# One accumulator per MLP tile, no weight remainders or norm squares on GpSimd, and another cost model for the order of the instructions

## The chip, the cores and the metric

The kernel runs on one core of one Trainium2 chip. The metric is the device time of one execution in microseconds (us), the median of several runs. A core has a matmul engine (TensorE, PE in the profile; its weight loads are shown apart as PEld), three engines for elementwise work (VectorE = DVE, ScalarE = ACT, GpSimd = POOL) and SyncE (SP), which here issues DMAs.

## The reference

The reference is a decoder trunk of two layers on 256 tokens of width 1024, in fp32:

```python
for layer in range(2):
    h = rms_norm(x, mix_norm[layer])
    if layer == 0:   # gated DeltaNet (8 heads x 64) beside a short gated convolution (512 channels)
        x = x + gdn_shortconv_mixer(h, w_in, qkv_conv, a_log, dt_bias, o_norm, sc_conv, w_out)
    else:            # native sparse attention, 16 heads, 4 key groups, three gated branches
        x = x + nsa_mixer(h, w_in, cmp_pos, k_w1, k_w2, v_w1, v_w2, w_out)
    h = rms_norm(x, mlp_norm[layer])
    x = x + square(relu(h @ w_up[layer])) @ w_down[layer]     # 1024 -> 4096 -> 1024
return rms_norm(x, final_norm)
```

The DeltaNet mixer projects, convolves q, k and v over time (width 4), applies SiLU, normalises q and k per head, inverts a triangular matrix per chunk and scans over chunks. The attention mixer projects, rotates a quarter of each head, compresses blocks of keys and values by a small MLP, and runs softmax over compressed, selected and window keys.

## The kernel before

**Weights and products.** All weights come as one stream of 108 MB or so, mostly in transfers of 1 MB, issued by SP into four slots called `st` (line 407). Each unit of a transfer (128 x 1024, in layer 0 also 512 and 528, for values 560) is split in two: ScalarE copies its high part `uh` (in the fp32r format that PE takes), and VectorE or GpSimd subtracts to get the exact remainder `ul` (`splits`, lines 443 to 451). Four buffers hold split units. X, the normalised input `x` and the MLP's hidden `U` are held as such pairs too. A product is then hi·xh + hi·xl + lo·xh. There are two forms of it. `mm256` issues three matmuls of 256 columns into one accumulator. `mm512` issues one matmul of 512 columns (xh and xl side by side) that fills both halves of a bank, and one of 256 columns for lo·xh; the two halves are added when the tile is evacuated (`addab`, line 623: ScalarE copies one half to `tb`, VectorE adds).

**Stages.** In the trace the layer-0 mixer takes 0 to 210 us, its MLP 210 to 381, the layer-1 mixer 381 to 553, its MLP 553 to 726, and the final norm and the store the rest. An MLP computes 32 up tiles (the first four contraction outermost in `proj_ko`, 28 one after the other in `proj_m`), then 8 down tiles of 32 products each. Its norm's factor is applied at the end: the square of it, `r2`, multiplies the down tiles.

**Norms.** When a tile of X is done, `Norm.ready` makes the pair `x`, squares the tile (`sq`, by ScalarE or GpSimd) and adds it to `nacc` (VectorE or GpSimd); `Norm.finish` sums over partitions by matmuls with `ones` and gets 1/rms.

**What sets the order.** Every engine runs its instructions in program order, and that order is made when the kernel is built. The work is written as generators (streams); the class `Order` always lets the stream go on that could start first by its clock. The clock goes by costs from `Timed.cost` (PE) and `Timed.other` (others), by a delay after each engine (`LAG`), and by a rule that doubles PE's cost after a stretch with few matmul columns (`TICK`, `BUSY`). Where a stream may choose an engine, the estimated end decides, with a bias in ns: `GB1` (first 16 units) and `GBIAS` favour GpSimd for remainders, `QBIAS` for squares. The costs are estimates for the order alone. All instructions but the DMAs issued at line 407 carry the line of the helper that records them, 279 before and 294 after.

## Time and profile before

| | |
|---|---|
| median of 3 runs | 741.78 us (738.81 to 750.28) |
| the profiled execution: span on the chip | 737.2 us |
| its own time | not recorded apart from the three runs; the median lies 4.6 us above its span |
| PE busy | 684.5 us in 5613 matmuls |
| DVE / ACT / POOL busy | 555.7 / 352.3 / 216.0 us |
| DMA | 108.94 MB, mean 148 GB/s |

The span is divided by engine and by stage in the rows below. Busy times add up over an engine's instructions; idle time on PE is what the stages differ in. The granted clock (PEclk) is given as a share of full speed, 1.00 for 2.4 GHz and 0.50 for 1.2 GHz.

### The profile page before, as it was taken

What the parts mean: (1) busy time and instruction counts of PE and PEld (TensorE: products, weight loads), DVE (VectorE), ACT (ScalarE), POOL (GpSimd) and SP (SyncE); (2) the same over time, 40 slices, a digit from 0 to 9 for tenths busy, and PEclk for the clock granted to TensorE, in tenths of its full rate; (3) what the DMA queues carried; (4) which work ended last, traced back from release to release, by engine and by line L of the source; (5) the groups of instructions that cost most, each with busy time, mean ns of one, the idle gap of its engine ahead of it and who ended that gap; (6) DMA issues with size and microseconds to landing.
All of it is one profiled execution on the core that took longest, in us unless ns stands there. A gap on an engine that the chain in (4) does not pass through costs nothing.

```text
span 737.2 us, 13951 instructions
## 1 busy us (share of the span) xinstructions
PE 684.5 (93%) x5613; PEld 602.5 (82%) x5613; DVE 555.7 (75%) x1007; ACT 352.3 (48%) x681; POOL 216.0 (29%) x229
## 2 busy tenths in 40 slices
PE   8878979999999999999999799888989999999994
PEld 6877878898888888888898677876778888888884
DVE  6999976676898887666679987798598888754552
ACT  6353423242656565444446647445655656544430
POOL 3536786512520000012143455342361000011211
PEclk9999999999999999999999989999999999999998
DMA  8552323113545554554552347412134555555401
GB/s 281 209 179 108 130 68 110 60 59 115 172 160 187 203 193 172 186 208 178 175 174 89 106 156 239 162 58 62 60 128 153 179 209 183 176 191 204 173 0 58
DMA packets 17633, 108.94 MB, mean 148 GB/s; under 512 B 2080, under 2 KB 2336, under 8 KB 5536
## 3 DMA queue, kind: packets, MB, share of 16 engines
q1 hardware_dynamic: 17280, 107.52, 41.8%
q8 instruction: 44, 0.72, 0.4%
q10 hardware_dynamic: 288, 0.52, 0.2%
q14 instruction: 21, 0.17, 0.1%
HBM read 106.99 MB, written 1.05 MB: 147 GB/s over the span
## 4 chain that ended last, share of the span: by engine, by line
PE 72%; DVE 22%; issue 3%; ACT 2%; DMA 1%; SPq 0%; POOL 0%; DVEq 0%; ACTq 0%
PE b L279 72%; DVE ul L279 4%; DVE cvconv L279 2%; DVE cm L279 1%; DVE rqt L279 1%; DVE x L279 1%; ACT uh L279 1%; DVE tt L279 1%; DVE qr L279 1%; DVE swq L279 1%; DMA X<-xt 1%; DVE nacc L279 1%; DVE X L279 1%; DVE ncol L279 1%; DVE qrot L279 1%
## 5 line engine op out<-in xcount | busy, mean ns | idle before, releaser
L279 ACT ACTIVATE uh<-st 128x1024 fp32r<-128x1024 f32 (+3 forms) x204 | 205.4, 1011 | 235.2 <-PE b L279 214.6
L279 PE MATMUL b<-x,uh 128*128 128x256 f32 (+1 forms) x1120 | 304.4, 348 | 1.7 <-DVE x L279 1.4
L279 DVE TENSOR_TENSOR ul<-st,uh 128x1024 fp32r<-128x1024 f32 (+3 forms) x166 | 205.3, 1238 | 102.5 <-ACT uh L279 101.5
L279 PE MATMUL b<-x,ul 128*128 128x256 f32 x832 | 227.1, 285 | 2.5 <-DVE ul L279 2.5
L279 PEld LDWEIGHTS b<-x,uh 128*128 128x128 f32 x1120 | 193.1, 195 | 24.3 <-DVE x L279 2.2
L279 PE MATMUL b<-U,uh 128*128 128x512 f32 (+1 forms) x576 | 179.8, 371 | 0.0
L279 PEld LDWEIGHTS b<-x,ul 128*128 128x128 f32 x832 | 160.9, 193 | 8.9 <-DVE ul L279 3.3
L279 PE MATMUL b<-U,ul 128*128 128x256 f32 x512 | 141.5, 281 | 0.0
L279 PEld LDWEIGHTS b<-U,uh 128*128 128x128 f32 x576 | 103.1, 188 | 19.5
L279 POOL TENSOR_TENSOR ul<-st,uh 128x1024 fp32r<-128x1024 f32 (+3 forms) x38 | 77.6, 2045 | 71.9 <-ACT uh L279 69.8
L279 PEld LDWEIGHTS b<-U,ul 128*128 128x128 f32 x512 | 96.1, 188 | 1.3
L279 POOL TENSOR_TENSOR nacc<-nacc,sq 128x256 f32<-128x256 f32 x24 | 28.8, 1200 | 70.3 <-ACT sq L279 69.3
L279 DVE TENSOR_TENSOR t<-b,tb 128x256 f32<-128x256 f32 x82 | 34.3, 418 | 0.1
L279 POOL TENSOR_TENSOR X<-X,par 128x256 f32<-128x256 f32 x8 | 5.6, 703 | 97.7 <-ACT nacc L279 90.5
L279 ACT ACTIVATE tb<-b 128x256 f32<-128x256 f32 x82 | 30.0, 369 | 7.6 <-PE b L279 6.5
L279 POOL TENSOR_TENSOR nacc<-X 128x256 f32<-128x256 f32 x2 | 1.2, 614 | 101.3 <-DVE X L279 101.3
L279 DVE SCALAR_TENSOR_TENSOR u<-t 128x256 f32<-128x256 f32 x64 | 29.2, 456 | 2.2
L279 ACT ACTIVATE px<-b,nm 128x128 f32<-128x128 f32 (+1 forms) x64 | 26.1, 429 | 8.9 <-DVE nm L279 8.8
L279 DVE TENSOR_TENSOR U<-u,U 128x256 fp32r<-128x256 f32 x64 | 28.2, 446 | 1.1 <-ACT U L279 1.1
L279 ACT ACTIVATE U<-u 128x256 fp32r<-128x256 f32 x64 | 25.7, 404 | 6.3 <-DVE u L279 6.2
L279 POOL TENSOR_TENSOR sq<-X 128x256 f32<-128x256 f32 x13 | 9.9, 765 | 64.0 <-DVE X L279 57.4
L279 DVE SCALAR_TENSOR_TENSOR x<-X,par,x 128x256 fp32r<-128x256 f32 x32 | 25.7, 831 | 3.6 <-ACT x L279 3.5
(277 smaller groups left out, 920.5 us busy)
## 6 DMA issues: line engine op xcount, KB each, us to landing
st<-wts SPq DMA_DIRECT2D x94, 1024.0 KB, 4.8
st<-wts SPq DMA_DIRECT2D x4, 560.0 KB, 3.7
st<-wts SPq DMA_DIRECT2D x4, 528.0 KB, 4.4
st<-wts SPq DMA_DIRECT2D x8, 256.0 KB, 5.8
X<-xt SPq DMA_DIRECT2D x3, 256.0 KB, 5.9
par<-par SPq DMA_DIRECT2D x1, 525.0 KB, 6.1
out_dram<-X SPq DMA_DIRECT2D x2, 256.0 KB, 2.5
out_dram<-X ACTq DMA_DIRECT2D x2, 256.0 KB, 3.1
```

The costliest lines, as they stand in the source:

```text
L279: r = f(*a, **k)
```

## The change

**MLP tiles.** Up and down tiles use `mm256` (three matmuls of 256 columns, one accumulator) throughout. An up tile was evacuated by a copy on ScalarE, an add and a relu-square on VectorE, the high part on ScalarE and the remainder on VectorE; now ScalarE does relu, square and high part, and VectorE the remainder alone. A down tile loses its copy and its add.

**GpSimd.** The choice of engine goes: remainders `ul` are always VectorE's, high parts and squares always ScalarE's. Thirty-eight remainders move from GpSimd to VectorE, thirteen squares and two first sums from GpSimd to ScalarE. The other work of GpSimd stays.

**Cost model.** `LAG` becomes a delay out of one engine (`OUT`), a delay into the next (`IN`) and a part by which neighbours on one engine overlap (`OVER`). All cost formulas get other numbers; a two-input VectorE instruction and a GpSimd instruction are kept apart in the model (`port`); `BUSY` goes from 3060 to 1500 and the assumed DMA rate from 360 to 330. Since the order is made from this, instructions move everywhere.

By kind of instruction: PE goes from 4792 to 5752 matmuls (512-column matmuls with `x` from 544 to 32 and with `U` from 448 to none); DVE from 997 to 888, ACT from 621 to 690, POOL from 234 to 182; SP's 122 stay.

```diff
-GBIAS, HBIAS, XBIAS, QBIAS, DBIAS = -1000, 1e9, 300, -300, -400
-GB1, QB0, XB0 = -600, 0.0, 1e9
+XBIAS, DBIAS, XB0 = 300, -400, 1e9
-TICK, BUSY = 10240 / 3, 3060.0
+TICK, BUSY = 10240 / 3, 1500.0
...
-    LAG = {None: 0.0, 'PE': 120.0, 'V': 130.0, 'A': 190.0, 'G': 130.0, 'D': 2000.0}
+    OUT = {None: 0.0, 'PE': 175.0, 'V': 10.0, 'A': 10.0, 'G': 10.0, 'D': 1200.0}
+    IN = {'PE': 43.0, 'V': 23.0, 'A': 23.0, 'G': 68.0, 'D': 60.0}
+    OVER = {'PE': 0.0, 'V': 80.0, 'A': 95.0, 'G': 40.0, 'D': 0.0}
...
-        c.t = self.free[eng] = start + cost
+        elif eng == 'G':
+            start = max(start, self.port[2])
+            self.port[:2] = start, start + cost
+        elif port:
+            if self.port[0] - cost < start < self.port[1]:
+                start = self.port[1]
+            self.port[2] = start + cost
+        c.t = start + cost
+        self.free[eng] = c.t - self.OVER[eng]
...
-        return max((0.8 if aps[2].dtype == F32R else 0.2) * m, n / (2.4 if m > 64 else 3.3)) + 2, n * rows / 128
+        return max((0.86 if aps[2].dtype == F32R else 0.25) * m, 0.46 * n), n * rows / 128
...
-            pick = yield dict(V=68 + 1.04 * n, G=160 + 2.09 * n + (GB1 if i < 16 else GBIAS))
-            (V if pick == 'V' else G).tensor_sub(lo[:, :n], src, hi[:, :n].bitcast(F32))
+            yield 'V'
+            V.tensor_sub(lo[:, :n], src, hi[:, :n].bitcast(F32))
...
-            pick = yield dict(A=307, G=687 + (QBIAS if self.idx else QB0))
+            yield 'A'
...
-            if pick == 'A':
-                A.activation(sq, X[:, m], AF.Square)
-            else:
-                G.tensor_mul(sq, X[:, m], X[:, m])
+            A.activation(sq, X[:, m], AF.Square)
...
-                yield from e.addab(acc, t)
+                A.activation(t, acc[:, :T], AF.Relu)
+                order.release(acc)
                 u = up.tile([128, T], F32, name="u", bufs=3)
-                V.scalar_tensor_tensor(u, t, 0.0, t, op0=OP.max, op1=OP.mult)
-                yield from e.hilo(U[:, base + m, 0], U[:, base + m, 1], u)
+                A.activation(u, t, AF.Square)
+                A.activation(U[:, base + m, 0], u, AF.Copy)
+                yield 'V'
+                V.tensor_sub(U[:, base + m, 1], u, U[:, base + m, 0].bitcast(F32))
...
-        yield from e.proj_ko(n, evac(0))
-        yield from e.proj_m(n.x, 28, evac(4), wide=True)
+        yield from e.proj_ko(n, evac(0), wide=False)
+        yield from e.proj_m(n.x, 28, evac(4))
...
-            if m < KT - 1:
-                yield from e.addab(acc, t)
-                V.tensor_mul(t, t, r2)
-            else:
-                yield 'V'
-                V.tensor_mul(t, acc[:, :T], r2)
-                order.release(acc)
+            yield 'V'
+            V.tensor_mul(t, acc[:, :T], r2)
+            order.release(acc)
...
-                if m < KT - 1:
-                    e.mm512(acc, hi[:, s], lo[:, s], U[:, k], k == 0, k == 31)
-                else:
-                    e.mm256(acc[:, :T], hi[:, s], lo[:, s], U[:, k, 0], U[:, k, 1], k == 0, k == 31)
+                e.mm256(acc[:, :T], hi[:, s], lo[:, s], U[:, k, 0], U[:, k, 1], k == 0, k == 31)
```

**Where instructions move.** On PE, in the layer-0 mixer, the matmuls with `lsq` (sums for the norm of k, made from the convolved k) stand between the projection matmuls of the next tiles. Before:

```order
L279 MATMUL b_584<-x,uh_506 128x256 x2
L279 MATMUL b_584<-x,ul_507 128x256
L279 MATMUL b_594<-par,lsq 128x2 x2
L279 MATMUL b_584<-x,uh_506 128x256 x2
L279 MATMUL b_584<-x,ul_507 128x256
```

And now:

```order
L294 MATMUL b_606<-x,uh_520 128x256 x2
L294 MATMUL b_606<-x,ul_521 128x256
L294 MATMUL b_617<-par,lsq 128x2 x2
L294 MATMUL b_606<-x,uh_520 128x256 x2
L294 MATMUL b_606<-x,ul_521 128x256
```

The first `lsq` follows 42 projection matmuls of this kind before and 66 now: it stands 24 matmuls later.

On DVE, the same place: `cvconv` is the convolution of a tile of k, `K` its result, `ul` a remainder. Before, the convolutions of one tile follow each other, and the remainders made meanwhile are GpSimd's:

```order
L279 SCALAR_TENSOR_TENSOR K<-K,cvconv 128x256
L279 TENSOR_TENSOR sp<-abn,par 128x16
L279 SCALAR_TENSOR_TENSOR ex<-sp 128x16
L279 MEMSET preconv 128x4
L279 TENSOR_TENSOR preconv<-b_538,rbc 128x256
L279 TENSOR_SCALAR cvconv<-preconv,par 128x256
L279 SCALAR_TENSOR_TENSOR cvconv<-preconv,par,cvconv 128x256 x3
```

And now:

```order
L294 TENSOR_SCALAR cvconv<-preconv,par 128x256
L294 TENSOR_TENSOR ul_480<-st,uh_479 128x1024
L294 SCALAR_TENSOR_TENSOR cvconv<-preconv,par,cvconv 128x256
L294 TENSOR_TENSOR ul_505<-st,uh_504 128x1024
L294 TENSOR_TENSOR ul_521<-st,uh_520 128x1024
L294 SCALAR_TENSOR_TENSOR cvconv<-preconv,par,cvconv 128x256
L294 TENSOR_TENSOR ul_544<-st,uh_543 128x1024
L294 SCALAR_TENSOR_TENSOR K<-K,cvconv 128x256
```

Four remainders of 128x1024 now stand between the steps of one convolution.

On PE, at the start of the last MLP (`proj_ko`, eight contraction steps for four tiles), the row sums of its norm (`ones,nacc`). Before, after the first tile's pairs of the last unit:

```order
L279 MATMUL b_6374<-x,ul_6395 128x256
L279 MATMUL b_6374<-x,uh_6394 128x512
L279 MATMUL b_6477<-ones,nacc 128x1 x2
L279 MATMUL b_6375<-x,ul_6395 128x256
L279 MATMUL b_6375<-x,uh_6394 128x512
```

And now, after all four tiles:

```order
L294 MATMUL b_6770<-x,uh_6776 128x256 x2
L294 MATMUL b_6770<-x,ul_6777 128x256
L294 MATMUL b_6928<-ones,nacc 128x1 x2
L294 MATMUL b_6931<-x,uh_6814 128x256 x2
L294 MATMUL b_6931<-x,ul_6815 128x256
```

Six more products (three tiles, two each) now stand ahead of it.

## Rows read from the trace of the kernel before

**Rows 1.** From the page: the span, the busy time of each engine, the granted clock over the span (40 slices, in tenths), and the shares of the engines in the chain that ended last.

```profile
span 737.2 us, 13951 instructions
...
PE 684.5 (93%) x5613; PEld 602.5 (82%) x5613; DVE 555.7 (75%) x1007; ACT 352.3 (48%) x681; POOL 216.0 (29%) x229
...
PEclk9999999999999999999999989999999999999998
...
PE 72%; DVE 22%; issue 3%; ACT 2%; DMA 1%; SPq 0%; POOL 0%; DVEq 0%; ACTq 0%
```

**Rows 2.** Busy time by stage: the stretch and its length in us, then PE, PEld, DVE, ACT and POOL busy (instructions), the mean granted clock, the share of the DMA engines, GB/s. The last row is a stretch of 20 us within the layer-0 mixer.

```profile
0.00:210.00 210.00, 184.94 (x2463) 169.70 (x2463) 168.19 (x328) 84.77 (x144) 105.39 (x105) 0.98 0.39 136
210.00:381.00 171.00, 170.85 (x1019) 150.82 (x1019) 126.52 (x187) 86.87 (x136) 19.57 (x22) 1.00 0.54 187
381.00:553.00 172.00, 154.13 (x1114) 128.70 (x1114) 141.41 (x297) 96.19 (x265) 74.31 (x87) 0.97 0.35 119
553.00:726.00 173.00, 172.98 (x1010) 152.06 (x1011) 115.42 (x183) 83.72 (x135) 14.84 (x14) 0.99 0.45 156
...
40.00:60.00 20.00, 14.92 (x111) 14.48 (x110) 19.06 (x42) 8.06 (x18) 9.32 (x6) 0.91 0.47 165
```

**Rows 3.** PE's timeline at the ends of uniform stretches: start in us, duration, instruction. From 557.34 to 635.74 stand 224 pairs of `mm512` with `x`; from 635.74 to 714.56 the pairs with `U` (seven down tiles, 448 matmuls); to 725.99 the last down tile as `mm256`, 95 steps. The two rows at 376 us are seven `mm256` triples with `x` apart.

```profile
376.26 0.40 PE L279 MATMUL b<-x,uh 128*128 128x256 f32 x2
378.79 0.40 PE L279 MATMUL b<-x,uh 128*128 128x256 f32 x2
557.34 0.48 PE L279 MATMUL b<-x,uh 128*128 128x512 f32 x1
635.74 0.39 PE L279 MATMUL b<-U,uh 128*128 128x512 f32 x1
714.56 0.63 PE L279 MATMUL b<-U,uh 128*128 128x512 f32 x3
725.99 0.28 PE L279 MATMUL b<-U,ul 128*128 128x256 f32 x1
```

**Rows 4.** POOL's remainders: its busy time with them in the two mixers (stretch, length, busy, count, clock, DMA), and all of them (duration ns min/median/max, first and last start in us, forms).

```profile
0.00:210.00 210.00, 38.67 (x19) 0.98 0.39 136
381.00:553.00 172.00, 33.51 (x17) 0.97 0.35 119
L279 POOL TENSOR_TENSOR ul<-st,uh x38: 1349/2365/2879, 11.4 to 558.5; 128x1024 fp32r<-128x1024 f32 x23, 128x560 fp32r<-128x560 f32 x7, 128x528 fp32r<-128x528 f32 x6, 128x512 fp32r<-128x512 f32 x2
```

**Rows 5.** Groups of DVE instructions by form (count, busy us, mean ns of one, idle before and its releaser): `cvconv`, `x` in the layer-0 mixer, `ul` from 220 to 290 us. Then the tile view of `cvconv`: ns min/median/max, first and last start.

```profile
L279 DVE SCALAR_TENSOR_TENSOR cvconv<-preconv,par,cvconv 128x256 f32<-128x256 f32 x24 | 21.0, 874 | 0.7
L279 DVE SCALAR_TENSOR_TENSOR x<-X,par,x 128x256 fp32r<-128x256 f32 x16 | 13.6, 884 | 3.6 <-ACT x L279 3.5
L279 DVE TENSOR_TENSOR ul<-st,uh 128x1024 fp32r<-128x1024 f32 x25 | 30.6, 1225 | 9.5 <-ACT uh L279 9.2
L279 DVE SCALAR_TENSOR_TENSOR cvconv<-preconv,par,cvconv x24: 478/485/2507, 26.0 to 73.9; 128x256 f32<-128x256 f32 x24
```

**Rows 6.** Timeline of DVE and POOL from 38 to 45 us: start, duration, instruction; in brackets the wait before it and what ended it.

```profile
38.43 5.01 POOL L279 TENSOR_TENSOR ul<-st,uh 128x1024 fp32r<-128x1024 f32 x2 [2.28 <-ACT uh L279]
38.68 2.50 DVE L279 TENSOR_SCALAR cvconv<-preconv,par 128x256 f32<-128x256 f32 x1
41.21 3.03 DVE L279 SCALAR_TENSOR_TENSOR cvconv<-preconv,par,cvconv 128x256 f32<-128x256 f32 x2
```

**Rows 7.** PE's longest wait for the convolution (timeline), and the three stretches in which the granted clock is 0.50 in the mixers and after them (columns as in Rows 2).

```profile
47.89 0.88 PE L279 MATMUL b<-par,lsq 128*128 128x2 f32 x4 [4.36 <-ACT lsq L279]
48.10:51.40 3.30, 3.30 (x18) 3.30 (x17) 3.23 (x5) 2.40 (x7) 1.86 (x1) 0.50 0.43 181
423.60:430.30 6.70, 5.54 (x23) 5.06 (x24) 6.36 (x16) 0.67 (x1) 2.37 (x2) 0.50 0.72 285
553.30:556.60 3.30, 3.30 (x13) 2.91 (x13) 2.46 (x12) 0.38 (x1) 0.00 (x0) 0.50 0.38 159
```

**Rows 8.** Timeline in the layer-1 mixer: POOL's two remainders, DVE's remainder of the same size, and PE's wait for the keys (`KD`, made by DVE from `t`).

```profile
420.08 2.78 POOL L279 TENSOR_TENSOR ul<-st,uh 128x560 fp32r<-128x560 f32 x2
423.53 0.74 DVE L279 TENSOR_TENSOR ul<-st,uh 128x560 fp32r<-128x560 f32 x1
424.76 0.55 PE L279 MATMUL b<-KD,qr 128*128 128x256 f32 x1 [4.54 <-DVE t L279]
```

**Rows 9.** Timeline at the end of the layer-1 mixer: a remainder on POOL, the last addition of the norm's squares on DVE, and PE's wait for it.

```profile
549.71 2.88 POOL L279 TENSOR_TENSOR ul<-st,uh 128x1024 fp32r<-128x1024 f32 x1 [0.74 <-ACT uh L279]
550.31 2.56 DVE L279 TENSOR_TENSOR nacc<-nacc,sq 128x256 f32<-128x256 f32 x1
553.02 0.78 PE L279 MATMUL b<-ones,nacc 128*128 128x1 f32 x4 [3.21 <-DVE nacc L279]
```

**Rows 10.** Groups of ACT instructions (count, busy us, mean ns): the copy out of a PSUM bank, the high part of `U`, and the high part of a 128x1024 unit.

```profile
L279 ACT ACTIVATE tb<-b 128x256 f32<-128x256 f32 x82 | 30.0, 369 | 7.6 <-PE b L279 6.5
L279 ACT ACTIVATE U<-u 128x256 fp32r<-128x256 f32 x64 | 25.7, 404 | 6.3 <-DVE u L279 6.2
L279 ACT ACTIVATE uh<-st 128x1024 fp32r<-128x1024 f32 x180 | 190.1, 1059 | 217.9 <-PE b L279 206.5 <-issue 6.6 <-POOL gt L279 2.7
```

More of the change, by code (lines that the diff above doesn't have):

```diff
@@ L194, in give, with _lag, spend @@
         self.tokens[name].append(self._now())
-    def spend(self, eng, cost, cols=0.0):
+    def _lag(self, s, eng):
+        return 0.0 if eng == s.last else self.OUT[s.last] + self.IN[eng]
+    def spend(self, eng, cost, cols=0.0, port=False):
         c = self.cur
-        start = max(self.free[eng], c.hold, c.t + (0.0 if eng == c.last and eng in ('PE', 'D') else self.LAG[c.last]))
+        start = max(self.free[eng], c.hold + self.IN[eng], c.t + self._lag(c, eng))
         if eng == 'PE':
@@ L220, in _start @@
         if isinstance(w, str):
-            return max(self.free[w], s.hold, s.t + (0.0 if w == s.last else self.LAG[s.last])), w
+            return max(self.free[w], s.hold + self.IN[w], s.t + self._lag(s, w)), w
         if isinstance(w, dict):
-            now = max(s.hold, s.t + self.LAG[s.last])
-            e = min(w, key=lambda e: max(self.free[e], now) + w[e])
-            return max(self.free[e], now), e
+            now = lambda e: max(self.free[e], s.hold + self.IN[e], s.t + self._lag(s, e))
+            e = min(w, key=lambda e: now(e) + w[e])
+            return now(e), e
         if w[0] == 'flag':
@@ L287, in cost @@
         if self.name != 'PE':
-            return (self.other(op, a, k, aps, size),)
+            return self.other(op, a, k, aps, size)
         rows = aps[1].shape[0]
@@ L301, in other @@
         if 'dma' in op:
[L302 to L303 removed]
+            return 60.0,
+        col = any(size(x) == 1 for x in aps[2:]) and n > 1
+        sbuf = sum(x.space != PSUM and size(x) > 1 for x in aps[1:])
         if self.name == 'V':
             if op == 'reciprocal':
[L306 removed]
+                return 150 + 6.4 * n,
             if op == 'memset':
[L308 to L310 removed]
+                return 58 + 0.8 * n, 0.0, True
+            if op in ('tensor_copy', 'tensor_scalar'):
+                quick = sbuf == 1 and aps[0].space != PSUM
+                return 150 + (0.55 if quick else 1.06) * n + 60 * col, 0.0, quick
+            return 155 + 1.05 * n + 60 * col, 0.0, sbuf > 1 and op not in ('transpose', 'stream_shuffle', 'tensor_reduce')
         if self.name == 'G':
             if op == 'memset':
[L313 removed]
+                return 90 + 0.9 * n,
             if op in ('tensor_scalar', 'tensor_copy'):
[L315 removed]
+                return 145 + 1.2 * n,
             col = any(list(x.ap)[-1][0] == 0 for x in aps)
[L317 removed]
+            return 180 + (1.68 if col else 2.12) * n,
         need = TABLES.get(a[2] if op == 'activation' else None)
```

30 lines of the change are left out of this document (10 added, 20 removed).

## The prediction

> **What bounds the kernel now.** I read the page first: PE is busy for 684.5 of 737.2 us, 93%, and holds 72% of the chain that ended last; DVE holds 22% of it [rows 1]. That is a mean over unlike stages, so the view by stage comes next [rows 2]. In both MLPs PE is never idle (170.85 of 171.00 us, 172.98 of 173.00): there only the price of a matmul counts. In the two mixers PE is idle for 210.00 − 184.94 = 25.1 us and 172.00 − 154.13 = 17.9 us, and the granted clock is 0.98 and 0.97; there DVE has 168.2 of 210 and 141.4 of 172 us, and 19.06 of 20 us in the stretch from 40 on. So the mixers are a shared matter of PE and DVE. To see what ends PE's waits I took the timeline at the three places that lose most and have a stretch of lower clock right behind them [rows 7 to 9].
>
> How far a time can move: the span is 737.2 us, the median of the runs 741.78, and I add these 4.6 us to every span worked out below. What a measurement of this kernel can tell from no change is about 2%, so "faster" means below 726.9 and "slower" above 756.6.
>
> **MLP tiles.** 512 products with `x` (2 MLPs, 32 tiles, 8 steps) and 448 with `U` (2 x 7 tiles x 32) change from two matmuls to three. A pair with `x` costs (635.74 − 557.34) / 224 = 0.350 us, a pair with `U` (714.56 − 635.74) / 224 = 0.352 us [rows 3]. A triple with `U`: the row at 714.56 joins one last matmul of 512 columns with the first two of 256, so the last tile starts some 0.24 us later, and its 95 steps to 725.99 take 0.118 us each, 0.353 us for three. A triple with `x` in the seven at 376 us takes (378.79 − 376.26) / 7 = 0.361 us, with more else going on. So the column count decides, not the number of matmuls: the change costs 448 x 0.001 = 0.4 us with `U`, and with `x` between 512 x 0.003 = 1.5 (if it goes as with `U`) and 512 x 0.011 = 5.6. I take **+5**, near the row with `x`, with ends +2 and +10 (the seven triples' price for `U` too).
>
> The evacuation is hidden either way. ScalarE gets per up tile one high part of a unit, relu, square and high part of U, which cost 1.06 + 0.37 + 0.40 + 0.40 = 2.23 us if the square is like the other copies of its size [rows 10]; PE needs 8 x 0.353 = 2.83 us for the tile. It fits with 0.6 us to spare, and units are split some tiles ahead. If that cover went, PE would wait for `uh` and pay the excess per tile; nothing in the rows suggests it. DVE, at 126.5 of 171 us, loses two instructions per up tile and one per down tile; it was no bound there, so that is worth nothing in itself.
>
> **Remainders off GpSimd, layer-0 mixer.** Nineteen remainders take POOL 38.67 us there and seventeen 33.51 us in layer 1 [rows 4]; the other two of 38 fall in the MLPs and cost nothing beside a DVE that idles. Their forms are 23 x 1024, 7 x 560, 6 x 528 and 2 x 512; the layer-1 ones are the seven of 560 and ten of 1024, which leaves eleven of 1024 and the eight small ones to layer 0. On DVE one of 1024 takes 1.225 us undisturbed [rows 5] and one of 560 takes 0.74 [rows 8]. So DVE gets 11 x 1.225 + 8 x 0.74 = 19.4 us at most.
>
> What it gets back is the time by which POOL lengthens it. The timeline shows this directly: beside two remainders of 5.01 us together, a `cvconv` step lasts 2.50 us and the next two 3.03 us [rows 6], where the median of the step is 0.485 [rows 5]. In the group the mean is 874 ns: 24 x (874 − 485) = 9.3 us lost; the sixteen `x` of the same shape have 884: 6.4 us if they would take 485 alone. Together 15.7 us from two groups; smaller groups add to it. So DVE's load changes by less than +3.7 us, and I take it as even.
>
> The Trainium skill, "SBUF — State Buffer", section "SBUF: two separate sides", says that the port pair which DVE and GpSimd share is held as an exclusive lock for a whole instruction, the other one blocking fully. The lengths of 2.50 beside 2.50 and of 3.03 = 2.5 + 0.5 agree with it. By that rule each removed remainder could free DVE of as much as its own duration, 38.67 us in layer 0 instead of my 15.7, a DVE relieved by 19 us on balance; the rows bear this out only in those two groups, so it stands as a rival below.
>
> What even load is worth is read at the place. PE waits 4.36 us for `lsq`, and right behind it the granted clock is 0.50 for 3.30 us, of which half is lost: 4.36 + 1.65 = 6.0 us [rows 7]. The convolution that `lsq` waits for is the one lengthened at 38.68 [rows 6]. Now `lsq` stands 24 matmuls later (24 x 0.118 = 2.8 us of cover), and POOL has no remainder there; but DVE has four of its own between the steps, 4 x 1.225 = 4.9 us, against 5.01 us of POOL. I take **−6**. Ends: −12, about half of PE's idle time in the stage; and +6, where the four remainders and the 3.7 us come on top, less the cover (4.9 + 3.7 − 2.8).
>
> **Layer-1 mixer.** DVE gets 7 x 0.74 + 10 x 1.225 = 17.4 us on 141.4 of 172, and again is relieved of lengthening. PE's dearest wait is 4.54 us for the keys, begun while POOL makes two remainders of 560 in 2.78 us [rows 8]; around it the clock is at 0.50 for 6.70 us, 3.35 lost [rows 7]. DVE would need 2 x 0.74 = 1.5 us for these two. The scores and softmaxes are interleaved differently with the projections now, which I can't price. I take **−5**, short of 4.54 + 3.35 = 7.9, with ends −12 (two thirds of the idle time) and +5 (a third of the 17.4 uncovered).
>
> **Into the last MLP.** The norm's last addition lasts 2.56 us beside a remainder on POOL of 2.88, and PE waits 3.21 us for it, then runs 3.30 us at 0.50 [rows 7, 9]: 3.21 + 1.65 = 4.9 us. Without POOL the addition takes about 0.49, as the `cvconv` step of its size does, so it ends 2.1 us earlier, and six products, 6 x 0.353 = 2.1 us, now stand ahead of the row sums. I take **−4** of −4.9 to 0. The squares that POOL made go to ScalarE, which is busy for 96.2 of 172 us [rows 2] and so takes them at nothing; if it were late there, part of this −4 would be kept.
>
> The tail has no edit of weight. DMA issues are the same 122 in the same order; moving the split from POOL can only change when a slot comes free, and the DMA share is at most 0.54 in any stage [rows 2].
>
> **Sum:** +5 − 6 − 5 − 4 = −10 on 737.2 = 727.2; with 4.6 us, **732 us**.
>
> **The rivals.**
>
> *PE's gaps close much more* (0.27). If a remainder blocks DVE wherever it meets it, and the new costs put the work in a better order, layer 0 gains 15, layer 1 gains 12, the boundary 5, the MLP costs 2: −30, and 712 us. For it: PE idles for 43 us in the mixers, more than this asks, and a block of full length is what the step of 2.50 us beside 2.50 shows [rows 6]. Against: much of the idle time is waits on chains (inversion, scan, softmax) that the edit does not shorten.
>
> *The new order costs what the port gives* (0.16). All instructions of the mixers move; waits of a few us elsewhere take the place of those removed, and the MLP's +5 stays: +2 to +13, so 744 to 755.
>
> *Slower: DVE becomes the bound of the mixers* (0.12). It is at 19.06 of 20 us from 40 on, gets 19.4 and 17.4 us more, and POOL's other work (105.4 − 38.7 = 66.7 us, 74.3 − 33.5 = 40.8 us) keeps lengthening its instructions. If the relief is only a quarter of the 15.7, DVE grows by 15 us in layer 0; if in layer 1 half of its 17.4 is uncovered, 8; the MLP adds 7: +30, and 772 us. It decides from the point where relief stays under about half of what is added. Against: the lengthened instructions that the timeline shows stand beside remainders [rows 6, 9], not beside POOL's other work.
>
> The Trainium skill, "Perfetto Trace Analysis", section "Optimizing Scalar/DVE Operations", speaks for neither side alone: a saturated DVE may be relieved by another engine, but between DVE and GpSimd moving work might not help, since they share a port.
>
> That the model reorders nothing of weight is not a case: the order of the rows above has moved.
>
> **How the numbers follow.** The forecast (span −3 to −17, so 725 to 739) has 0.45, and 732 is its middle; the three rivals have 0.27, 0.16 and 0.12. The range takes in the forecast, the first rival's 712 with some room, and the second rival up to 755; it leaves out the slower rival and some of the far ends: **708 to 755**. Faster by over 2% is the first rival plus the forecast's edge below 726.9 (0.06): 0.33. Slower is its rival: 0.12. Within 2% is the rest, 0.55.
>
> **What would show it.** Right: the MLP stages at 0.353 to 0.361 us per product, 2 to 6 us longer in all and PE still without idle; `cvconv` and `x` near 0.49 us in the mean; the wait for `lsq` and its stretch at 0.50 gone or halved; the addition of squares below 1 us. Wrong: an MLP up phase in which PE waits for `uh` or the evacuation; a new wait in the mixers that DVE's `ul` ends last and that is longer than those removed; DVE instructions still at over twice their median, beside other work of POOL.

## The result and the profile after

The changed kernel takes 709.81 us (median of 4 runs, 708.28 to 711.95), the kernel before 740.81 beside it. The ratio is 0.958, 95% interval 0.954 to 0.962: faster, by 31 us. The forecast was 732 us; the first rival, PE's gaps closing much more, stood at 712. The profiled run took 711.32 us, 1.8 us above its span of 709.5.

The page of the changed kernel, its totals and chain (they answer to [rows 1]):

```profile
PE 679.1 (96%) x6573; PEld 640.3 (90%) x6573; DVE 478.9 (67%) x898; ACT 388.3 (55%) x750; POOL 134.9 (19%) x177
...
PE 82%; DVE 11%; issue 3%; ACT 2%; DMA 1%; SPq 0%; POOL 0%; DVEq 0%; ACTq 0%; POOLq 0%
```

PE's busy time falls by 5.4 us; the other 22 us of the span are idle time of PE that is gone. DVE's share of the chain halves, and DVE is busy 77 us less, although it makes 38 more remainders. The table by stage puts 58 us of that in the two MLPs, where it lost instructions, and 18 us in the mixers.

For a clean cut by stage I set the borders where PE's work changes: the first product of each MLP, its last one, and the last of the layer-1 mixer. Busy time by stage, columns as in [rows 2], first the kernel before:

```profile
0.00:193.10 193.10, 170.01 (x2379) 157.12 (x2380) 151.66 (x305) 73.37 (x125) 94.79 (x97) 0.97 0.39 135
193.10:376.20 183.10, 180.97 (x1064) 158.60 (x1064) 139.88 (x204) 95.72 (x152) 26.93 (x23) 1.00 0.52 184
376.20:539.90 163.70, 149.29 (x1102) 125.66 (x1102) 131.60 (x290) 91.60 (x258) 68.47 (x88) 0.97 0.35 120
539.90:726.10 186.20, 182.72 (x1064) 160.01 (x1064) 128.39 (x196) 90.86 (x147) 23.93 (x21) 0.99 0.44 153
```

And the changed kernel:

```profile
0.00:185.60 185.60, 169.65 (x2379) 156.62 (x2380) 140.60 (x323) 74.89 (x129) 63.67 (x77) 0.96 0.41 140
185.60:366.30 180.70, 180.43 (x1544) 179.98 (x1543) 109.53 (x136) 112.08 (x184) 12.33 (x12) 1.00 0.55 187
366.30:517.70 151.40, 147.04 (x1103) 122.59 (x1103) 124.27 (x301) 93.68 (x263) 39.49 (x70) 0.99 0.37 131
517.70:698.40 180.70, 180.42 (x1544) 179.97 (x1543) 100.28 (x126) 106.81 (x175) 17.53 (x18) 1.00 0.45 158
```

The stages change by −7.5, −2.4, −12.3 and −5.5 us; the tail stays. In the layer-0 mixer POOL is busy 31.1 us less and DVE 11.1 us less, in the layer-1 mixer DVE is 7.3 us less busy, although it makes more remainders in both. How many shows in the same stretch of layer 0, with remainders alone: DVE and then POOL before, then DVE in the changed kernel.

```profile
0.00:193.10 193.10, 34.04 (x29) 0.97 0.39 135
0.00:193.10 193.10, 33.78 (x17) 0.97 0.39 135
...
0.00:185.60 185.60, 51.18 (x46) 0.96 0.41 140
```

With these borders seventeen remainders, 33.78 us of POOL, go over to DVE and cost it 17.1 us. Its other work is thus 11.1 + 17.1 = 28.2 us shorter. (The prediction counted nineteen and 38.67 us, because its stretch of 0 to 210 us reaches 17 us into the MLP; its second stretch, 381 to 553 us, reaches 13 us into the other. By the borders here five of the 38 remainders fall outside the mixers, not two.)

The same stretches with PE's products with `x` alone (first two rows, first and second MLP) and with `U` alone (last two) show the price of the MLP's matmuls. Before:

```profile
193.10:376.20 183.10, 90.42 (x512) 1.00 0.52 184
539.90:726.10 186.20, 91.82 (x512) 0.99 0.44 153
...
193.10:376.20 183.10, 90.30 (x544) 1.00 0.52 184
539.90:726.10 186.20, 90.36 (x544) 0.99 0.44 153
```

And after:

```profile
185.60:366.30 180.70, 93.06 (x768) 1.00 0.55 187
517.70:698.40 180.70, 93.04 (x768) 1.00 0.45 158
...
185.60:366.30 180.70, 87.01 (x768) 1.00 0.55 187
517.70:698.40 180.70, 87.05 (x768) 1.00 0.45 158
```

The triples with `x` cost more than the pairs (+2.6 us an MLP), the triples with `U` less (−3.3 us). The 91.82 holds the stretch at clock 0.50, for which 1.65 us are taken off below [rows 7]; against the first MLP it is 1.4 us longer.

Last, the rows of the changed kernel at the places of [rows 5] to [rows 9]: two DVE groups up to 210 us, PE's first `lsq`, a product with the keys, then the last addition of squares and the row sums behind it. The last two rows are new: PE's longest wait now, for the output `o` of the scan in the layer-0 mixer, and the stretch at clock 0.50 in which it ends.

```profile
L294 DVE SCALAR_TENSOR_TENSOR cvconv<-preconv,par,cvconv 128x256 f32<-128x256 f32 x24 | 13.6, 582 | 0.0
L294 DVE SCALAR_TENSOR_TENSOR x<-X,par,x 128x256 fp32r<-128x256 f32 x16 | 7.7, 508 | 3.3 <-ACT x L294 3.3
...
40.72 0.50 PE L294 MATMUL b<-par,lsq 128*128 128x2 f32 x4
...
407.78 0.80 PE L294 MATMUL b<-KD,qr 128*128 128x512 f32 x2 [0.28 <-DVE t L294]
...
529.34 0.43 DVE L294 TENSOR_TENSOR nacc<-nacc,sq 128x256 f32<-128x256 f32 x1 [0.63 <-POOL nacc L294]
529.91 0.58 PE L294 MATMUL b<-ones,nacc 128*128 128x1 f32 x4
...
169.29 1.09 PE L294 MATMUL b<-par,o 128*128 128x128 f32 x4 [4.58 <-DVE o L294]
167.20:177.40 10.20, 7.27 (x31) 6.61 (x32) 3.59 (x9) 2.05 (x3) 0.00 (x0) 0.50 0.30 101
```

The wait of 4.36 us for `lsq` is gone, the 4.54 us for the keys are 0.28, the addition takes 0.43 us instead of 2.56, and PE does not wait for it. `cvconv` has 582 ns in the mean instead of 874, `x` 508 instead of 884; for `cvconv` that is still above the 0.49 that the prediction named as the sign. The wait for `o` was 1.49 us before, and the clock was at 1.00 there. The changed kernel pays 4.58 us for it, and about half of the 7.27 us of work at clock 0.50 comes on top: some 8 us.

### The profile page after: what moved, and what is told of

Same layout as the page of the kernel before. It is cut to its first block, busy times and chain, and to the rows that moved or that the text cites. A ratio compares the mean times of both kernels' runs of the same rounds, so it can differ in the third digit from the quotient of the medians.

```text
span 709.5 us, 15854 instructions
## 1 busy us (share of the span) xinstructions
PE 679.1 (96%) x6573; PEld 640.3 (90%) x6573; DVE 478.9 (67%) x898; ACT 388.3 (55%) x750; POOL 134.9 (19%) x177
## 4 chain that ended last, share of the span: by engine, by line
PE 82%; DVE 11%; issue 3%; ACT 2%; DMA 1%; SPq 0%; POOL 0%; DVEq 0%; ACTq 0%; POOLq 0%
PE b L294 82%; DVE ul L294 3%; DVE cvconv L294 1%; DMA X<-xt 1%; DVE kc L294 1%; ACT uh L294 1%; DVE rqt L294 0%; ACT px L294 0%; DVE lc L294 0%; SPq L425 0%; DVE o L294 0%; DVE qr L294 0%; DVE al L294 0%; POOL px L294 0%; DVE nm L294 0%
## 5 line engine op out<-in xcount | busy, mean ns | idle before, releaser
L294 DVE TENSOR_TENSOR ul<-st,uh 128x1024 fp32r<-128x1024 f32 (+3 forms) x204 | 244.2, 1201 | 154.6 <-ACT uh L294 152.6
L294 PEld LDWEIGHTS b<-x,uh 128*128 128x128 f32 x1632 | 257.4, 193 | 6.5 <-ACT uh L294 1.5
L294 PE MATMUL b<-U,uh 128*128 128x256 f32 x1024 | 174.2, 276 | 0.0
L294 PEld LDWEIGHTS b<-U,uh 128*128 128x128 f32 x1024 | 154.3, 188 | 0.0
L294 ACT ACTIVATE u<-t 128x256 f32<-128x256 f32 x64 | 26.7, 417 | 2.0
L294 POOL TENSOR_TENSOR px<-px,den 128x128 f32<-128x128 f32 x32 | 17.4, 571 | 53.7 <-DVE den L294 39.3
L294 PE MATMUL b<-ohl,uh 128*128 128x256 f32 x128 | 25.2, 294 | 0.2
L294 PE MATMUL b<-uh,x 128*128 128x264 f32 (+1 forms) x128 | 24.8, 289 | 0.0
L294 ACT ACTIVATE t<-b 128x256 f32<-128x256 f32 x64 | 23.5, 367 | 0.0
L294 PEld LDWEIGHTS b<-ohl,uh 128*128 128x128 f32 x128 | 19.8, 189 | 0.9 <-ACT ohl L294 0.3
```

Of the source, the lines that this page charges most:

```text
L294: r = f(*a, **k)
```

## The experiments

All times below are medians, with the ratio to the kernel before in the same job.

**The three parts alone.** The change has an MLP part, a GpSimd part and a new cost model. Three kernels have one part each.

`only_mlp`, the kernel before with the MLP part (the evacuations too, as in the change):

```diff
-        yield from e.proj_m(n.x, 28, evac(4), wide=True)
+        yield from e.proj_m(n.x, 28, evac(4))
...
-                    e.mm512(acc, hi[:, s], lo[:, s], U[:, k], k == 0, k == 31)
...
+                e.mm256(acc[:, :T], hi[:, s], lo[:, s], U[:, k, 0], U[:, k, 1], k == 0, k == 31)
```

> The kernel before with one part of the change: one accumulator per MLP tile and the evacuation on ScalarE; remainders and squares may still go to GpSimd and the old cost model sets the order. Theory A (the MLP got cheaper because a triple of 256 columns with U costs 0.340 us, as in the trace of the changed kernel, and a triple with x 0.360): 448 x (0.340 - 0.352) = -5.4 us with U and 512 x (0.360 - 0.350) = +5.1 with x, so about 0, and PE's steps with U at 113 ns. Theory B (the prediction's price: a triple with U costs 0.353 as in the last tile of the kernel before, and the cheaper price belongs to something else in the change): +5 us, steps with U at 118 ns.

Measured: 737.73 us, ratio 0.997 (0.994 to 1.000). Theory A holds: products with `U` take 86.95 and 86.99 us as in the changed kernel, those with `x` 93.00 in the first MLP (95.56 in the second, whose granted clock is 0.98).

`only_gpsimd`, the kernel before with the GpSimd part:

```diff
-            pick = yield dict(V=68 + 1.04 * n, G=160 + 2.09 * n + (GB1 if i < 16 else GBIAS))
-            (V if pick == 'V' else G).tensor_sub(lo[:, :n], src, hi[:, :n].bitcast(F32))
+            yield 'V'
+            V.tensor_sub(lo[:, :n], src, hi[:, :n].bitcast(F32))
...
-            pick = yield dict(A=307, G=687 + (QBIAS if self.idx else QB0))
+            yield 'A'
...
```

> The kernel before with one part of the change: no remainders and no norm squares on GpSimd; MLP tiles and cost model as before. Theory A (GpSimd's remainders block VectorE for their full length, and that made most of PE's idle time in the mixers): 15 to 20 us faster than before, cvconv and x near 0.49 us in the mean, PE idle in the mixers cut by half. Theory B (VectorE is then the bound of the mixers, and it is the new cost model that puts the work in an order that hides it): no gain or some us slower, -3 to +10 us.

Measured: 722.74 us, ratio 0.976 (0.973 to 0.979), 18 us faster. Its two mixers and its `cvconv` group:

```profile
0.00:188.40 188.40, 168.51 (x2379) 155.51 (x2380) 145.42 (x323) 73.69 (x128) 61.73 (x77) 0.95 0.39 138
...
369.60:524.80 155.20, 147.11 (x1103) 122.33 (x1102) 126.43 (x304) 93.44 (x261) 40.68 (x68) 0.99 0.37 127
...
L279 DVE SCALAR_TENSOR_TENSOR cvconv<-preconv,par,cvconv 128x256 f32<-128x256 f32 x24 | 14.8, 615 | 0.6
```

Theory A in the main: no new model is needed for it. DVE is 6.2 and 5.2 us less busy than before in the two mixers, with all remainders on it; in layer 0 these take 50.89 us instead of 34.04, so its other work is 23.1 us shorter. But `cvconv` has 615 ns in the mean and not 0.49 us, and PE's idle time falls by half only in the layer-1 mixer (14.4 to 8.1 us); in layer 0 it goes from 23.1 to 19.9.

`only_model`, the changed kernel with the other two parts undone; the diff shows the biases alone, which I set anew to get near 38 remainders on GpSimd under the new costs (39 went there):

```diff
+GBIAS, HBIAS, XBIAS, QBIAS, DBIAS = -800, 1e9, 300, -300, -400
+GB1, QB0, XB0 = -450, 0.0, 1e9
...
```

> The changed kernel with two parts undone: two-half accumulators in the MLP and about as many remainders and squares on GpSimd as before, in the order that the new cost model makes. Theory A (the port: the gain in the mixers is the absence of GpSimd's remainders): within 5 us of before. Theory B (the order): 15 us or more faster than before, with the waits for lsq and for the keys gone.

Measured: 746.8 us, ratio 1.009 (1.007 to 1.012). While GpSimd makes remainders the new order is no gain but 6 us slower; theory B falls. Why it is slower was not followed further. Alone, the three parts give −3, −18 and +6 us; together they give −31, so half of the gain comes from their meeting.

**All but one part.** `all_but_model` is the kernel before with the edits of `only_mlp` and `only_gpsimd` together.

> The kernel before with the MLP and the GpSimd parts of the change, in the order of the old cost model. If the new model is worth nothing by itself: about 710 us as the changed kernel. If it makes the order that hides VectorE's added remainders: 15 us or more slower than the changed kernel, 725 to 740, with VectorE's remainders as what PE waits for in the mixers.

Measured: 720.56 us, ratio 0.974 (0.970 to 0.977), 11 us slower than the changed kernel. So the new model does pay once GpSimd's remainders are gone, somewhat less than expected.

`all_but_gpsimd` is the changed kernel with the choice of GpSimd put back, with the biases above:

```diff
-            yield 'V'
-            V.tensor_sub(lo[:, :n], src, hi[:, :n].bitcast(F32))
+            pick = yield dict(V=155 + 1.05 * n, G=180 + 2.12 * n + (GB1 if i < 16 else GBIAS))
+            (V if pick == 'V' else G).tensor_sub(lo[:, :n], src, hi[:, :n].bitcast(F32))
...
```

> The changed kernel with one part undone: about as many remainders and squares as before may go to GpSimd (33 of 38 remainders), in the order of the new cost model, with the new MLP tiles. If GpSimd's remainders are the cost (19 us in the run with that part alone): 25 to 35 us slower than the changed kernel, 735 to 745, with cvconv and x in the mixers at 0.8 to 0.9 us in the mean. If the new model's rule that keeps the two engines apart is what counts: within 10 us of the changed kernel.

Measured: 742.78 us, ratio 1.001 (0.998 to 1.004): 33 us slower than the changed kernel. The whole gain hangs on this part. Its `cvconv` group has 843 ns in the mean, as expected, its `x` only 564. Layer 0 has 17 us of the loss; there PE is busy 178.0 us at a granted clock of 0.89, 8 us more than in the changed kernel at 0.96, so part of what the remainders cost is paid in clock.

**What GpSimd does to VectorE.** `dummy_pool` leaves the remainders where the change put them and gives GpSimd idle work.

```diff
             V.tensor_sub(lo[:, :n], src, hi[:, :n].bitcast(F32))
+            if i % 2 == 0 and (4 <= i < 42 or 108 <= i < 140):
+                for _ in range(2):
+                    nc.gpsimd.tensor_sub(junk, hi[:, :384].bitcast(F32), hi[:, 128:512].bitcast(F32))
```

> The changed kernel, order unchanged on PE, VectorE and ScalarE, with idle work added on GpSimd: for 19 units in the layer-0 mixer and 16 in the layer-1 mixer two subtractions of 128x384 of the unit's high part into a tile that nobody reads, some 2 us a unit, about as long as the remainders that GpSimd made before. VectorE still makes all remainders. Theory A (GpSimd's two-input work blocks VectorE, whatever it computes): VectorE's cvconv and x groups lengthen to 0.7 us or more in the mean, and the kernel gets 10 to 25 us slower. Theory B (what cost the time before was that a unit came late from the slower engine, or GpSimd's queue): no group of VectorE lengthens, under 5 us.

Measured: 752.21 us, ratio 1.017 (1.014 to 1.020), 42 us slower than the changed kernel, with the same instructions on PE, VectorE and ScalarE, in the same order but for two neighbours on VectorE. Its mixers by stage, its `cvconv` group, the added work, and a `cvconv` step beside it:

```profile
0.00:210.70 210.70, 176.39 (x2379) 162.81 (x2380) 162.26 (x323) 74.75 (x129) 109.08 (x116) 0.93 0.36 123
...
391.30:558.30 167.00, 153.31 (x1102) 126.05 (x1101) 141.50 (x302) 93.48 (x263) 81.56 (x100) 0.95 0.33 120
...
L294 DVE SCALAR_TENSOR_TENSOR cvconv<-preconv,par,cvconv 128x256 f32<-128x256 f32 x24 | 19.9, 844 | 0.0
...
L471 POOL TENSOR_TENSOR junk<-uh 128x384 bf16<-128x384 f32 x70 | 96.2, 1375 | 85.6 <-ACT uh L294 82.6
...
35.05 2.23 POOL L471 TENSOR_TENSOR junk<-uh 128x384 bf16<-128x384 f32 x2 [2.83 <-ACT uh L294]
35.19 1.23 DVE L294 SCALAR_TENSOR_TENSOR cvconv<-preconv,par,cvconv 128x256 f32<-128x256 f32 x1
```

Work that nobody waits for lengthens VectorE by 21.7 us in the layer-0 mixer and 17.2 in the other (162.26 − 140.60, 141.50 − 124.27), and the stages by 25 and 16 us. Theory A holds for `cvconv`, at 844 ns; the group `x` of this stage only goes to 545, and the loss is more than the 10 to 25 us expected. In the layer-0 mixer PE waits longest for VectorE's remainders, 7.9 us in all. A part of the loss is GpSimd's own queue: PE waits 4.5 us for `gt` of GpSimd. Another part is the clock: 0.93 instead of 0.96 in layer 0, where PE is busy 6.7 us longer. The added work, 96.2 us, is more than the 72 us of the remainders in the mixers [rows 4], so its 42 us are no measure of theirs.

`only_remainders` takes the remainders off GpSimd and leaves the squares.

```diff
...
-            (V if pick == 'V' else G).tensor_sub(lo[:, :n], src, hi[:, :n].bitcast(F32))
...
+            V.tensor_sub(lo[:, :n], src, hi[:, :n].bitcast(F32))
```

> The kernel before with the 38 weight remainders off GpSimd and nothing else; its norm squares may stay there (12 do), MLP tiles and cost model as before. If the remainders carry the gain of the run without both: 719 to 724 us as that one (722.7). If the squares carry a part, as the wait for the last addition before the last MLP suggests: 3 to 6 us slower than that run, with that wait still near 3 us.

Measured: 724.49 us, ratio 0.978 (0.974 to 0.982). The remainders carry the gain; what the squares add (1.8 us) is not told from none. PE's wait for the last addition before the last MLP is down to 1.06 us, though squares stay on GpSimd.

**Which part of the new model.** `no_port` takes out the rule that keeps the two engines apart, `old_busy` puts one number back:

```diff
-        elif eng == 'G':
-            start = max(start, self.port[2])
-            self.port[:2] = start, start + cost
-        elif port:
-            if self.port[0] - cost < start < self.port[1]:
-                start = self.port[1]
-            self.port[2] = start + cost
```

```diff
-TICK, BUSY = 10240 / 3, 1500.0
+TICK, BUSY = 10240 / 3, 3060.0
```

> The changed kernel with the port rule taken out of the cost model (the delays, costs and BUSY stay new), so that a GpSimd instruction and a two-input VectorE instruction may stand side by side in the model. If this rule makes the new order's gain of 9 us over the old model: 716 to 722 us, with the mixers' VectorE groups longer. If the delays and costs make it: within 3 us of the changed kernel's 709.8.

> The changed kernel with BUSY back at 3060 (so that the model doubles PE's cost after most stretches of the mixers); everything else stays. If this rule makes the new order's gain: 716 to 722 us. If not: within 3 us of 709.8.

Measured: `no_port` 708.5 us, ratio 0.956 (0.953 to 0.960), no different from the changed kernel in total. `old_busy` 721.03, ratio 0.973 (0.970 to 0.977): the 11 us are lost. The two mixers, first in `no_port`, then in `old_busy`:

```profile
0.00:178.80 178.80, 168.66 (x2380) 156.73 (x2381) 140.02 (x322) 74.58 (x129) 63.10 (x77) 0.97 0.42 145
359.30:514.30 155.00, 147.79 (x1104) 124.02 (x1103) 124.82 (x299) 95.51 (x267) 38.16 (x68) 0.98 0.36 128
...
0.00:189.60 189.60, 169.45 (x2380) 157.38 (x2381) 143.17 (x322) 74.67 (x129) 62.29 (x77) 0.95 0.40 137
370.30:526.30 156.00, 148.98 (x1102) 123.00 (x1101) 124.81 (x299) 94.71 (x264) 38.80 (x71) 0.99 0.36 127
```

The changed kernel takes 185.6 and 151.4 us there. So the equal total of `no_port` hides two effects: the rule on the port costs 6.8 us in layer 0 and gives 3.6 back in layer 1. Each stage is read from one profiled run, and the runs of these kernels lie 3 to 5 us apart; but `up_pairs` and `up_pairs_no_port` below repeat it (186.7 and 150.3 us with the rule, 178.2 and 155.2 without). `old_busy` loses 4.0 us in layer 0 and 4.6 in layer 1.

`old_costs_new_busy` turns it round: `all_but_model` with BUSY = 1500.

> The kernel before with the MLP and the GpSimd parts of the change and, of the new cost model, BUSY = 1500 alone; delays and costs stay old. It is 720.6 with BUSY = 3060. If BUSY alone makes the further gain, as its undoing in the changed kernel cost 11 us: 708 to 712. If BUSY pays only together with the new delays and costs: 717 to 724.

Measured: 713.74 us, ratio 0.966 (0.962 to 0.970), between the two forecasts: of the 11 us that the new model gives, BUSY alone gives 7 by the medians, 6 by the ratios. By stage the profiled runs show 191.1 to 183.3 us in layer 0 and no change in layer 1 (155.5 both). So one number of the model is worth half of it or more by itself, and all of it when taken back. The rest lies in layer 1, and there every kernel with one part of the model at its old state, BUSY, the port rule or the costs and delays, takes 155.0 to 156.0 us instead of 151.4.

**The price of a product.** Products with `U` took 0.353 us as triples in the last tile of the kernel before [rows 3] and 0.340 here, from the same buffers. Two kernels change the values; `neg_zero` makes -0.0 for 0, `no_relu` leaves the relu out:

```diff
...
-                A.activation(u, t, AF.Square)
...
+                V.scalar_tensor_tensor(u, t, 0.0, t, op0=OP.max, op1=OP.mult)
...
```

```diff
-                A.activation(t, acc[:, :T], AF.Relu)
+                A.activation(t, acc[:, :T], AF.Copy)
```

> The changed kernel, but U is made as before, by VectorE as max(t, 0) * t, which gives -0.0 wherever t is negative, where relu and then the square give +0.0; the products, the banks and the addresses are the changed kernel's. Theory A (PE's pace depends on the values that it streams): a triple with U at 353 ns, as the last tile of the kernel before, the down phases 90.0 us instead of 86.7. Theory B (the pace comes from the form of the matmuls or from what else runs): 340 ns and 86.7 us.

> The changed kernel with the relu left out of the MLPs (so U = t squared and holds no zeros, another function than the reference's). Theory A (values): a triple with U slower than 340 ns, near the 360 of a triple with x, whose values are dense too; the down phases 90 to 92 us. Theory B (form, or the phase): 340 ns.

Measured: the products with `U` take 86.92 and 86.94 us in the first, 87.01 and 86.95 in the second (one run each, 713.89 and 712.99 us). These changes of the values do not move the price; theory A falls.

`pairs_plus` has the pairs of the kernel before in both halves of the MLP, and makes `U` thus (against the kernel before, other lines left out):

```diff
-                V.scalar_tensor_tensor(u, t, 0.0, t, op0=OP.max, op1=OP.mult)
+                V.tensor_scalar(t, t, 0.0, None, op0=OP.max)
+                A.activation(u, t, AF.Square)
```

> The changed kernel with the two-half accumulators and pairs of 512 and 256 columns in the MLP again, but with U's zeros positive: VectorE adds the halves and takes max with 0, ScalarE squares. Theory A (values decide the pace of U, the form that of x): x pairs at 350 instead of 360 ns, so the up phases 91.3 instead of 94 us; U pairs at 340 or below instead of 353, the down phases 86.7 or less; 5 us faster than the changed kernel, about 705. Theory B (the triple is the cheaper form for U): U pairs at 353, 710 to 712 in all.

Measured: 712.53 us, ratio 0.959 (0.953 to 0.964). Products with `x` take 90.42 and 90.50 us, with `U` 90.34 and 90.22. Theory B: for `U` the triple is the cheaper form here, for `x` the pair.

Next the place of the operands. By the built programs the weights' buffers and `x` start on multiples of 128 bytes and `U` 64 bytes past one; no trace shows these addresses, the runs show only what a shift of 64 bytes does. `swap` moves both by 64 bytes (the first line), `x64` moves `x` by 64 and `U` by 128 (both lines):

```diff
+    actp.tile([128, 16], F32, name="pad")
...
+        up.tile([128, 16], F32, name="pad")
```

> The changed kernel with x and U moved by 64 bytes in each partition, by a pad tile ahead of x: x then starts 64 bytes past a multiple of 128 bytes and U on a multiple, the other way round than in the changed kernel; the weights' buffers stay on multiples. Theory A (the pace of a product depends on where its moving operand lies against the weights): a triple with x at 340 ns instead of 360, one with U at 360 instead of 340. Theory B (it does not): 360 and 340 as before.

> The changed kernel with x moved by 64 bytes and U by 128 bytes in each partition, so that both start 64 bytes past a multiple of 128 bytes. Theory A (place against the weights): triples with x and U both at 340 ns, 512 x 0.020 = 10 us faster in the two up phases, and some us in the mixers, so 697 to 702. Theory B: no change, 708 to 712.

`lock` adds to `x64` a pad in each mixer, so that the operands just ahead of each MLP start on multiples:

```diff
+        p1.tile([128, 24], F32, name="pad")
         AL = [small(f"al{c}", 8, 128) for c in range(2)]
...
+        p1.tile([128, 16], F32, name="pad")
         KC = p1.tile([128, 2, 4, 128], F32, name="kc", tag="px1_4")
```

> The changed kernel with x and U moved so that both start 64 bytes past a multiple of 128 bytes, while the moving operands of the output projections ahead of each MLP (ya, yb, ohl) start on multiples. In the traces so far a stretch with U at 64 took 340 ns a triple whenever it followed a steady stretch at 360 with its operand on a multiple, and 353 or 340, whichever the stretch before had, when it followed one at 64. Theory A (the pace at 64 is set on entry and kept): x at 340 in both up phases, 5 us less each than the changed kernel, 698 to 701. Theory B (any interruption can set it anew): x at 353 or 340 by chance, runs spread between 698 and 712 as with x64.

Measured: `swap` 713.62 us (one run); `x64` 709.15, with runs of 697.91, 706.68, 711.61 and 712.89, all at a granted clock of 0.98; `lock` 713.03 (712.9 to 713.65), ratio 0.963. Products with `x` and then with `U` alone, first in `swap`, then `x64`, then `lock`; the two rows of each are the two MLPs:

```profile
182.60:366.70 184.10, 91.33 (x768) 1.00 0.53 183
516.30:700.60 184.30, 91.55 (x768) 1.00 0.44 155
...
182.60:366.70 184.10, 91.98 (x767) 1.00 0.53 183
516.30:700.60 184.30, 92.03 (x767) 1.00 0.44 155
```

```profile
183.80:366.30 182.50, 91.42 (x768) 1.00 0.54 185
517.10:693.40 176.30, 88.64 (x768) 1.00 0.46 162
...
183.80:366.30 182.50, 90.33 (x767) 1.00 0.54 185
517.10:693.40 176.30, 86.91 (x767) 1.00 0.46 162
```

```profile
183.60:366.10 182.50, 90.34 (x768) 1.00 0.55 185
517.40:699.90 182.50, 90.34 (x768) 1.00 0.44 156
```

The place counts: `U` on a multiple costs 92.0 us (360 ns a triple), 64 bytes past one 87.0 or 90.3 (340 or 353). `x` goes from 93.0 to between 91.3 and 91.6 when moved (in `lock`, whose rows above are those of `U`, too), and to 88.6 in one MLP of `x64`. Within a stretch the price does not drift, but it can change where other matmuls come between. PE's timeline at the start of the first MLP of `lock` shows it with `x`, on the same instructions and places: three triples at 353 ns, four at 340 behind the row sums of the norm, and three at 353 again behind two matmuls with `ncol`.

```profile
194.10 0.40 PE L294 MATMUL b<-x,uh 128*128 128x256 f32 x2
...
195.16 0.40 PE L294 MATMUL b<-x,uh 128*128 128x256 f32 x2
...
195.75 0.58 PE L294 MATMUL b<-ones,nacc 128*128 128x1 f32 x4
...
196.62 0.39 PE L294 MATMUL b<-x,uh 128*128 128x256 f32 x2
...
197.98 0.39 PE L294 MATMUL b<-x,uh 128*128 128x256 f32 x2
...
198.49 0.40 PE L294 MATMUL b<-par,ncol 128*128 128x128 f32 x2
...
199.08 0.40 PE L294 MATMUL b<-x,uh 128*128 128x256 f32 x2
...
200.14 0.40 PE L294 MATMUL b<-x,uh 128*128 128x256 f32 x2
```

In the second MLP of `x64` the pace goes from 353 to 340 ns behind the two matmuls with `ncol` at 532.12 us and stays there, through `U` as well. So theory B of `lock` holds: an interruption can set the pace anew, and the place of the operand in the stretch ahead does not decide it, though the four runs of `lock` do not spread as theory B had it (`x` comes in at 353 behind the output projection in `lock` as in `x64`). Which of the two paces an interruption leaves behind stays open.

**Versions that beat both kernels.** `up_pairs` uses each form where it is cheaper, pairs for the up tiles and triples for the down tiles:

```diff
-        yield from e.proj_ko(n, evac(0), wide=False)
-        yield from e.proj_m(n.x, 28, evac(4))
+        yield from e.proj_ko(n, evac(0))
+        yield from e.proj_m(n.x, 28, evac(4), wide=True)
...
+                yield from e.addab(acc, t)
+                V.tensor_scalar(t, t, 0.0, None, op0=OP.max)
+                yield 'A'
```

> The changed kernel with pairs of 512 and 256 columns for the up tiles alone (two halves, added by VectorE, max with 0 there too, square on ScalarE); the down tiles keep the triples. If a price goes with the form and the operand alone: up phases 91.7 instead of 93.9 us, down phases 86.7, and 4 to 5 us faster than the changed kernel, 705. If the pace of the triples with U hangs on what ran before them (they took 353 ns behind pairs with U in the kernel before): down phases 90, no gain.

Measured: 706.32 us, ratio 0.954 (0.950 to 0.957): products with `x` 90.40 and 90.53, with `U` 86.94 and 86.91 us. `up_pairs_no_port` also leaves the port rule out:

> The changed kernel with both parts that ran faster than it: pairs of 512 and 256 columns for the up tiles alone (706.3 by itself) and no port rule in the cost model (708.5 by itself). If they add up: 704 to 706. If the new order of the mixers eats one of them: 707 to 712.

Measured: 703.25 us (701.8 to 705.66), ratio 0.951 (0.948 to 0.954), lower than either in the median, though its runs overlap those of `up_pairs` (703.08 to 707.34). It is better than the changed kernel: its highest run is below the lowest of that.

## Why the prediction was wrong

The forecast was faster but too small: 732 against 709.8 us, of which 727.2 against 709.5 is span. The direction and most of the places were right; the sizes failed, above all in two terms, the layer-1 mixer (off by 7.3 us) and the MLP tiles (6.1 us), before the boundary (2.8) and layer 0 (1.5). By its own terms:

- **MLP tiles, +5, measured −1.1.** The term with `x` was right: 186.1 us against 182.2 − 1.65, +5.5. The term with `U` failed. "0.353 us for three" came from the last tile of the kernel before, 96 matmuls behind 448 others; in the changed kernel a triple with `U` takes 0.340, and the two down phases 6.6 us less than before. (A pair with `U`, counted to where the last tile starts, is 0.353 and not 0.352 us; that is worth 0.5 us.) "So the column count decides" is wrong: the operand's place counts, the form with it, and at one place an interruption can change the pace.
- **Into the last MLP, −4, measured −6.8.** Each MLP's stage holds time beyond its products, waits and matmuls of the norm: 2.4 and 4.0 us before, 0.6 and 0.6 after; with the 1.65 us of half clock that is −6.8. The prediction looked at the second MLP alone, which gives −5.1 of it; the first lost 1.8 us there too.
- **Layer-0 mixer, −6, measured −7.5.** Right in size, in good part by luck: two misses cancel. "I take it as even" was wrong: DVE's load fell by 11.1 us. Against that stands a wait that no term had, the one for `o` with the clock behind it, some 8 us. `no_port` has no such wait, and there the stage takes 178.8 us, 14.3 less than before. `only_gpsimd` has 4.7 of the 7.5 us from GpSimd, with a wait of 6.6 us for `o`.
- **Layer-1 mixer, −5, measured −12.3.** This is the largest miss: 8.5 us of it come with the GpSimd part alone (163.7 to 155.2), the other 3.8 with the new model as a whole, and I had priced one wait and refused the rest ("which I can't price").
- **4.6 us from span to median.** The profiled run of the changed kernel took 1.8 us more than its span, and the runs of all kernels here 1.7 to 2.2; a median of three runs against the span of one had made it 4.6.

The failing step common to both mixers is the relief of VectorE. I summed the lengthening of two groups, 15.7 us, and set it against 19.4 us of added remainders. VectorE's busy time in layer 0 shows 17.1 us added and 11.1 less in all, so 28.2 us of relief, and 23.1 with the GpSimd part alone, for 33.78 us of remainders taken off GpSimd.

The sentence that named the Trainium skill, "SBUF — State Buffer", section "SBUF: two separate sides", would have come nearer: by an exclusive lock for the whole instruction, up to the full duration of the remainders could be freed, as an estimate from that rule. The trace agrees in direction; the relief is 68% (GpSimd part alone) to 83% (changed kernel) of that bound.

The first rival rested on this and gave −30 in the span (measured −27.7). Its total came near partly by errors that cancel: its parts were −15, −12, −5 and +2, measured −7.5, −12.3, −6.8 and −1.1.

The slower rival fell with `only_gpsimd`: the relief is not under half of what is added, but more than all of it. The page "Perfetto Trace Analysis", section "Optimizing Scalar/DVE Operations", in the Trainium skill says that moving work between the two engines might not help; here it decided the case, in the direction off GpSimd (`all_but_gpsimd`: 33 us).

What was not foreseen at all is that one constant of the cost model is worth 11 us (`old_busy`). In the layer-0 mixer PE's wait for `o` shows a good part of where: 6.6 us in `old_busy` and in `all_but_model`, 4.6 in the changed kernel, 0.4 in `old_costs_new_busy`, none in `no_port`. The stage takes 189.6, 191.1, 185.6, 183.3 and 178.8 us in these five. That the smaller BUSY places this work better is measured; by which decisions was not tried.

## What to carry to other kernels

When one engine's work lengthens another's, as GpSimd's did VectorE's here, price a move between them by both engines' busy time in the stage: sum what every instruction of the hindered engine loses, or bound it by the other engine's whole duration, not by the groups that stand out. A price for a new form of matmul should come from a long stretch with the same operand in the same place, and where there is none, both ends belong in the range. In an order made by a cost model, undo its constants one by one, and read the result by stage: here one number was worth half or more, and the elaborate rule, worth nothing in total, lost 7 us in one stage and gave 4 back in another.

## What was not expected of the hardware

The same matmul (128 columns of weights, 256 moving columns, granted clock 1.00) has three paces. With the moving operand's start on a multiple of 128 bytes, as the weights, a triple takes 360 ns (93.0 us for 256 triples and their starts in an up phase, 92.0 for a down phase); 64 bytes past it 353 or 340 (90.3 or 86.9 us). The last two can follow each other in one phase: a few other matmuls in between are enough, in `lock` at 195.75 and again at 198.49 us. `x64` spread over 15 us from run to run, and its profile has one MLP at 353 and one at 340 in the products with `U`.

What sets 340 or 353 at one place stays open: the two changes of the values left 340 as it was, and the operand's place in the stretch ahead does not decide it.
